# One transfer over 128 partitions in place of two over 64, for four tiles of the neighbourhood heads

## The chip, the cores and the metric

The kernel runs on one core of one Trainium2 chip. The metric is the device time of one execution in microseconds, median of several runs. The engines are TensorE (PE; its weight loads are listed as PEld), VectorE (DVE), ScalarE (ACT), GpSimd (POOL) and SyncE (SP). In this kernel SP computes nothing: its queue issues the transfers that the program asks for, one after the other, and 16 DMA engines carry them out.

## What is computed

The reference is one layer of a diffusion trunk: a SwiGLU half step, two attentions on one normalised input (neighbourhood attention and latent attention) that are merged through gates, and a second SwiGLU half step. The change touches the neighbourhood attention alone. For each of its 8 heads, each of 1024 latent queries attends in one softmax to a window of a 16 x 64 grid, with a relative bias, and to all 256 context tokens:

```python
qg, kg, vg = grid(q * d ** -0.5), grid(k), grid(v)
...
s_loc = jnp.einsum('bjqhd,bjakhd->bhjqak', q_r, k_b).astype(jnp.float32) + bias.astype(jnp.float32)
s_loc = jnp.where(valid[:, :, None, :], s_loc, neg).reshape(B, H, n_blk, NA_QCOLS, n_loc)
s_ctx = jnp.einsum('bjqhd,bkhd->bhjqk', q_r, k_ctx).astype(jnp.float32)
p = jax.nn.softmax(jnp.concatenate([s_loc, s_ctx], axis=-1), axis=-1).astype(v.dtype)
p_loc = p[..., :n_loc].reshape(B, H, n_blk, NA_QCOLS, kh, NA_KCOLS)
o = (jnp.einsum('bhjqak,bjakhd->bjqhd', p_loc, v_b)
     + jnp.einsum('bhjqk,bkhd->bjqhd', p[..., n_loc:], v_ctx))
```

A head is 64 wide (`d`). Everything is float32.

## The kernel before

To reach float32 accuracy, the kernel splits each operand into a high and a low part. A head is only 64 wide, and TensorE contracts over 128 partitions, so the two parts of a key lie one above the other: partitions 0 to 63 of the tile `k` hold the high part of the keys, 64 to 127 the low part. The tile `q` holds the high part of the queries twice, in both halves, and `ql` their low part twice. So `q` against `k` gives high times high plus high times low in one matmul. `kvc[:, 0:256]` holds the context keys, high over low like `k`.

An earlier stage computes these operands and stores them in DRAM scratch: `qas[i]`, of shape [2, 128, 1024], has the high and low queries of the two heads 2i and 2i+1, and `kas[i]`, of shape [2, 128, 1280], their keys, the last 256 columns being those of the context (L1363 and L1364). `NaHead.loads` (L1719) brings them back, head by head. It is a generator with four stages, and `na_next(h, n)` (L1885) moves it on:

- first, `q`, `ql`, the context keys and `k` (L1721 to L1730), and bias table 0;
- then bias table 1 and two blocks of values (one tile `va`);
- then bias table 2 and the context values;
- then two more blocks of values (one tile `vb`).

A head is worked off in four items (`NaItem`, L1972), one for each block of 16 grid columns. An item's `scores` (L1976) multiplies `q` and `ql` by `kvc` and by `k` into PSUM, adds the bias on VectorE and takes the maxima; its exponentials follow on ScalarE; its `values` transposes the probabilities on TensorE and multiplies them by the values.

The order is written out by hand, and each engine keeps it. Step n of the main loop (L2230) issues the three value parts of item n and between them the scores of item n + 3 (`AHEAD`). The scores of items 0 to 2 (`EARLY`) already run in the projection stage before. The first loads of head h + 1 are issued in the program at step 4h (`ahead_head`, L2190), the rest as its items 0 and 2 are created (`na_item`, L2150). Heads 0 and 1 are loaded out of the planned stage before (L1913, L1914).

Buffers limit how far the loads run ahead. The pool `w` has six tiles for `q`, `ql` and `k`: two heads. `kvc` lies in one of two `kc` tiles, or for every third head in `x`. Bias tables have three tiles (`y`), and values go round five tiles (of `l`, `p` and `z`). Every transfer is issued by SP in program order (`ld`, L122, and `put`, L131, at L132), so a load that waits for its buffer holds back all that stand behind it in SP's queue. Stores of the projection stage (`d<-t` in the views) stand in the same queue.

After the 8 neighbourhood heads the same loop works off 8 latent heads (`MlaHead`, L2060), whose loads the change doesn't touch.

## Time and profile before

| | us |
|---|---|
| median of 3 runs | 2557.08 |
| lowest and highest run | 2555.43 and 2558.92 |
| span of the profiled execution, first to last instruction | 2553.0 |

The profiled execution's own time is its span and what lies around it; the median of the runs is 4.1 us above the span. In the page, the 40 slices are of 63.8 us each. The neighbourhood heads are loaded and worked off between about 1289 and 1475 us, in slices 21 to 24. TensorE was granted its full clock throughout (0.999).

In the views, `w` stands for the tiles `q`, `ql` and `k` of a head, `kc` and `x` for its context keys, `y` for bias tables, `p`, `z` and `l` for values, `d` for DRAM scratch and `t` and `xu` for tiles of 512 and 1024 columns. KB are of 1024 bytes, MB and GB of powers of ten. All transfers are issued at line L132, the helper.

### The profile page before, as it was taken

The numbers are of one execution on the slowest core, as the hardware profiler recorded it, in microseconds if no ns is written. First come the engines' busy times: TensorE is split into PE (matmuls) and PEld (weight loads), VectorE is DVE, ScalarE is ACT, GpSimd is POOL, SyncE is SP. The second block draws the span as 40 slices with busy tenths as digits, with TensorE's granted clock in tenths as the row PEclk, the third lists the DMA queues.
The fourth block names the chain that finished last, engine by engine and source line by source line (L and its number), as shares of the span: only waits on it lengthen the run. The fifth ranks groups of instructions, "written<-read, shape, count | busy, mean of one in ns | idle before, by whom it ended". The sixth has DMA issues, their size and how long they took to land.

```text
span 2553.0 us, 38188 instructions
## 1 busy us (share of the span) xinstructions
PE 2524.7 (99%) x13007; PEld 2146.5 (84%) x13007; DVE 1904.4 (75%) x3652; ACT 1238.4 (49%) x2384; POOL 239.4 (9%) x421
## 2 busy tenths in 40 slices
PE   8999999999999999999999999999999999999998
PEld 6888888888888888889889999988888888888887
DVE  5788887898567687874568988886445888777557
ACT  6622223555346643433438888772355322233633
POOL 1000000000002200001006622220030000000000
PEclk9999999999999999999999999999999999999999
DMA  8477765779576665666899823205135667557655
GB/s 314 161 244 234 243 224 188 274 247 294 182 241 221 245 224 188 226 229 203 277 284 249 233 67 77 77 28 214 67 131 179 212 223 236 183 185 259 240 202 194
DMA packets 275477, 523.33 MB, mean 205 GB/s; under 512 B 33425, under 2 KB 84433, under 8 KB 275281
## 3 DMA queue, kind: packets, MB, share of 16 engines
q1 hardware_dynamic: 275280, 520.88, 61.3%
q8 instruction: 103, 1.69, 0.3%
q14 instruction: 94, 0.76, 0.1%
HBM read 375.47 MB, written 145.29 MB: 204 GB/s over the span
## 4 chain that ended last, share of the span: by engine, by line
PE 87%; ACT 5%; DVE 4%; issue 2%; DMA 1%; SPq 0%; POOL 0%; DVEq 0%; POOLq 0%; ACTq 0%
PE bs L161 33%; PE bm L161 30%; PE bv L161 20%; PE bm L164 2%; ACT xu L2105 2%; PE bs L164 1%; DVE xu L1966 1%; DVE t L2132 1%; ACT t L2131 1%; ACT xu L2004 1%; DVE xv L120 1%; DMA xv<-in_wada 0%; ACT t L2105 0%; ACT t L1938 0%; PE bv L164 0%
## 5 line engine op out<-in xcount | busy, mean ns | idle before, releaser
L120 ACT CAST xu<-t 128x512 fp32r<-128x512 f32 x589 | 345.6, 618 | 669.8 <-DVE t L120 556.1
L161 PE MATMUL bm<-xu,xu 128*128 128x512 f32 (+1 forms) x2442 | 596.5, 389 | 0.5 <-ACT t L120 0.4
L161 PEld LDWEIGHTS bm<-xu,xu 128*128 128x128 f32 x2442 | 450.4, 188 | 91.6 <-ACT t L120 1.7
L120 DVE TENSOR_TENSOR xu<-t,xu 128x512 fp32r<-128x512 f32 x589 | 382.8, 686 | 78.3 <-ACT xu L120 78.0
L161 PE MATMUL bs<-xu,xu 128*128 128x512 f32 (+2 forms) x1581 | 388.4, 385 | 0.0
L161 PE MATMUL bs<-xv,xu 128*128 128x512 f32 x1512 | 363.6, 390 | 0.2 <-DVE t L120 0.2
L161 PEld LDWEIGHTS bs<-xu,xu 128*128 128x128 f32 x1581 | 291.9, 188 | 57.8
L161 PE MATMUL bv<-xv,xu 128*128 128x512 f32 x1342 | 336.1, 390 | 0.0
L161 PEld LDWEIGHTS bs<-xv,xu 128*128 128x128 f32 x1512 | 283.6, 188 | 59.5 <-issue 1.0
L161 PEld LDWEIGHTS bv<-xv,xu 128*128 128x128 f32 x1342 | 251.7, 188 | 51.9
L120 DVE TENSOR_TENSOR xu<-xu,xu 128x512 fp32r<-128x512 f32 x282 | 189.5, 687 | 59.9 <-ACT xu L120 58.9
L120 DVE TENSOR_TENSOR t<-t,t 128x512 f32<-128x512 f32 (+4 forms) x350 | 221.0, 634 | 13.9 <-ACT t L120 8.7
L161 PE MATMUL bv<-xu,xu 128*128 128x512 f32 x722 | 191.5, 390 | 0.0
L120 ACT CAST xu<-xu 128x512 fp32r<-128x512 f32 x282 | 169.2, 619 | 15.2 <-DMA xu<-in_f1w 8.9
L120 POOL TENSOR_SCALAR st<-st 128x1 f32<-128x1 f32 x56 | 23.8, 425 | 1581.9 <-ACT t L120 1234.4
L161 PEld LDWEIGHTS bv<-xu,xu 128*128 128x128 f32 x722 | 135.6, 188 | 28.0
L161 PE MATMUL bm<-t,xu 128*128 128x256 f32 (+1 forms) x920 | 156.9, 333 | 0.0
L161 PEld LDWEIGHTS bm<-t,xu 128*128 128x128 f32 x920 | 137.7, 189 | 18.3
L161 PE MATMUL bs<-w,w 96*128 96x512 f32 (+1 forms) x384 | 145.0, 406 | 3.9 <-DVE st L1995 2.1
L2132 DVE TENSOR_TENSOR t<-bm,t 128x512 fp32r<-128x512 f32 x160 | 109.6, 687 | 28.5 <-ACT t L2131 28.1
L164 PE MATMUL bm<-ident,xu 128*128 128x128 f32 x826 | 126.5, 272 | 0.0
L1966 DVE TENSOR_SCALAR_CACHE_REDUCE xu<-bs 128x512 f32<-128x512 f32 (+1 forms) x186 | 110.2, 599 | 2.3 <-PE bs L161 2.1
(256 smaller groups left out, 3376.3 us busy)
## 6 DMA issues: line engine op xcount, KB each, us to landing
d<-t SPq DMA_DIRECT2D x432, 256.0 KB, 2.9
t<-d SPq DMA_DIRECT2D x348, 256.0 KB, 4.9
xu<-in_f1w SPq DMA_DIRECT2D x104, 512.0 KB, 4.4
xu<-in_f2w SPq DMA_DIRECT2D x58, 512.0 KB, 4.6
t<-in_wada SPq DMA_DIRECT2D x112, 256.0 KB, 4.9
t<-in_f1w SPq DMA_DIRECT2D x77, 256.0 KB, 4.8
t<-in_f2w SPq DMA_DIRECT2D x77, 256.0 KB, 5.2
xu<-in_winT SPq DMA_DIRECT2D x36, 512.0 KB, 5.4
```

Of the source, the lines that this page charges most:

```text
L120: return lambda *x, **y: pin(f(*x, **y))
L161: return pin(nc.tensor.matmul(o, s, m, start=start, stop=stop, skip_group_check=open_group[0]))
L164: return pin(nc.tensor.transpose(o, x, i))
L1966: nc.vector.tensor_scalar(dst, src, 1.0, FMIN, op0=ALU.mult, op1=ALU.max, accum_out=m)
L2004: soft.append(lambda s=s: nc.scalar.activation(pr[s][:, :640], pr[s][:, :640], AF.Exp, bias=n_[:, s:s + 1], accum_out=l[:, s:s + 1]))
L2105: nc.scalar.activation(x, x, AF.Exp, bias=n_[:, s:s + 1], accum_out=l[:, i:i + 1])
L2131: nc.scalar.copy(t[0], pb)
L2132: nc.vector.tensor_tensor(t[1], pb, f32(t[0]), op=ALU.subtract)
```

## The change

```diff
             self.kvc = kvc = W(key="x" if h % 3 == 2 else "kc")
-            for s in range(2):
-                o = 64 * s
-                ld(f32(q[o:o + 64, :]), qas[i][0, b:b + 64, :])
-                ld(f32(ql[o:o + 64, :]), qas[i][1, b:b + 64, :])
-                ld(f32(kvc[o:o + 64, 0:256]), kas[i][s, b:b + 64, NLAT:])
-            for s in range(2):
-                ld(f32(k[64 * s:64 * s + 64, :]), kas[i][s, b:b + 64, :NLAT])
+            for s, x in enumerate((q, ql)):
+                ld(f32(x), qas[i][s:s + 1, b:b + 64, :].to_broadcast([2, 64, NLAT]))
+            ld(f32(kvc[:, 0:256]), kas[i][:, b:b + 64, NLAT:])
+            ld(f32(k), kas[i][:, b:b + 64, :NLAT])
             self.bias = []
             self.table(0)
```

Eight transfers a head become four. The same bytes land in the same places. Each new transfer writes all 128 partitions of a tile from a source of three dimensions, two by 64 by the columns. For `q` and `ql` the outer dimension of two is a repetition: the same 64 rows are read twice. For `k` and the context keys it goes from the high part to the low part in `kas`. The order changes a little: the context keys' transfer used to be the third and the sixth, and is now the third of four, ahead of `k`.

## The prediction

> **What bounds the kernel now.** I read the page first, for the whole and for the place of the change:

> ```profile
> span 2553.0 us, 38188 instructions
> ...
> PE 2524.7 (99%) x13007; PEld 2146.5 (84%) x13007; DVE 1904.4 (75%) x3652; ACT 1238.4 (49%) x2384; POOL 239.4 (9%) x421
> ...
> DMA  8477765779576665666899823205135667557655
> GB/s 314 161 244 234 243 224 188 274 247 294 182 241 221 245 224 188 226 229 203 277 284 249 233 67 77 77 28 214 67 131 179 212 223 236 183 185 259 240 202 194
> ```

> TensorE is busy for 99% of the span: overall it sets the time. But slices 21 to 23 (1276 to 1467 us) have their DMA engines at 8 to 9 tenths, and that is where the neighbourhood heads are loaded. So the second view is that of the windows: a stretch at the start in which the DMA engines are saturated by whole tiles, and the stretch of the heads.

> ```profile
> core 0: us, PE busy (x) PEld busy (x) DVE busy (x) ACT busy (x) POOL busy (x), PEclk, DMA share, GB/s
> 3.00:43.00 40.00, 32.73 (x307) 24.00 (x308) 17.51 (x37) 20.41 (x37) 3.83 (x4) 1.00 1.03 397
> 1310.00:1450.00 140.00, 133.10 (x987) 126.91 (x986) 119.66 (x408) 112.67 (x267) 81.14 (x156) 1.00 0.92 247
> 1344.00:1445.00 101.00, 94.58 (x747) 92.32 (x746) 92.37 (x318) 90.67 (x221) 71.15 (x134) 1.00 0.98 256
> ```

> Two readings. TensorE idles for 140 - 133.1 = 6.9 us in the heads' 140 us, so nothing that only makes loads quicker can gain more than that here. And the DMA engines are as busy as can be (0.98) though they move only 256 GB/s, against 397 GB/s at the start: some transfers of this stage are slow for their size. The stage is balanced between TensorE and the DMA engines, so a change of either kind could show.

> Third, the timeline of SP's queue and of TensorE's weight loads, and the views of waits, tell how early the loads come:

> ```profile
> 1288.80 1.14 SPq L132 DMA_DIRECT2D w<-d  x2
> ...
> 1307.42 1.25 SPq L132 DMA_DIRECT2D w<-d  x2
> ...
> 1345.41 1.09 SPq L132 DMA_DIRECT2D w<-d  x2
> ...
> 1358.80 1.43 SPq L132 DMA_DIRECT2D w<-d  x2
> ```

> ```profile
> 1309.75 0.31 PEld L161 LDWEIGHTS bs<-kc,w 128*128 128x128 f32 x2
> ...
> 1355.86 0.30 PEld L161 LDWEIGHTS bs<-x,w 128*128 128x128 f32 x2
> 1358.09 0.30 PEld L161 LDWEIGHTS bs<-w,w 128*128 128x128 f32 x2 [1.92 <-DVE t L2027]
> ...
> 1373.12 0.30 PEld L161 LDWEIGHTS bs<-kc,w 128*128 128x128 f32 x2
> 1389.57 0.30 PEld L161 LDWEIGHTS bs<-kc,w 128*128 128x128 f32 x2
> ...
> 1437.18 0.30 PEld L161 LDWEIGHTS bs<-kc,w 128*128 128x128 f32 x2
> ```

> ```profile
> PE bs L161 <- DMA w<-d: 1.7, 1, 1.7
> ...
> SPq L132 <- DMA w<-d: 14.6, 21, 1.3
> ```

> Heads 0 to 3 are first loaded at 1288.80, 1307.42, 1345.41 and 1358.80 and first used at 1309.75 (head 0), 1355.86 (head 2), 1373.12 (head 3), 1389.57 (head 4) and 1437.18 (head 7). From head 3 on a head takes (1437.18 - 1373.12) / 4 = 16.0 us, and its load has 1373.12 - 1358.80 = 14.3 us to land. TensorE waited once for `w`, 1.7 us, at head 2: there is slack, but of 10 to 14 us only. SP in turn waits 21 times for landings of `w`, so its issues cannot run far ahead of slow transfers.

> **The change part by part.**

> *Issues.* Eight become four a head. SP gives about 0.6 us to each (two in 1.14 to 1.43 us), so its queue is relieved by some 2.4 us a head. SP is off the chain here. Should the three-dimensional source make an issue dearer, even twice 0.6 us leaves the sum as it was. I count nothing, either way.

> *Bytes.* They stay: 3 x 512 KB for `q`, `ql`, `k` and 128 KB of context keys, 1664 KB a head.

> *Engines.* Each new transfer has an outermost source dimension of 2 where the old ones had 64 rows. No transfer of before has one so small, so the price must be bounded. Shape does matter to speed here: the window above needs 0.98 of 16 engines for 256 GB/s. A head's other loads are 3 x 384 + 4 x 256 + 128 = 2304 KB, all over 128 partitions; at 397 GB/s they take 5.9 us of the 16.0 x 0.98 = 15.7 us that the engines are busy, which leaves 9.8 us for the 1664 KB in 64-row transfers, 174 GB/s, less than half of what whole tiles get. If a transfer is dealt to the engines by its outermost dimension, the source of 2 can be dealt to two engines and no more: one copies the upper half, the other the lower. One engine carries 397 / 16 = 24.8 GB/s. The bounds are 16 engines (1664 KB in 4.3 us, quicker than now) and 2 engines at that rate. I take two engines, since the outermost dimension is what the edit changes and the nearest rows, those of 64-row transfers, already show that fewer outer rows cost speed with all engines occupied.

> [...]

> *The sum.* On each of the two engines, a head's own load is 3 x 64 rows of 4096 bytes at 24.8 GB/s, 3 x 10.6 us, and 64 rows of 1024 bytes, 2.6 us: 34.3 us. All four transfers use the same two engines and follow each other. Those two also carry their sixteenth of everything else:

> ```profile
> q1 hardware_dynamic: 16417, 35.75, 92.4%
> ...
> w<-d SPq DMA_DIRECT2D x48, 256.0 KB, 7.3
> y<-in_bias SPq DMA_DIRECT2D x21, 384.0 KB, 5.5
> d<-t SPq DMA_DIRECT2D x24, 256.0 KB, 4.3
> ```

> ```profile
> t<-d SPq DMA_DIRECT2D x10, 128.0 KB, 2.2
> ```

> The first fence is the view of transfers in the window from head 0's first load to head 7's last, 1288.7 to 1428.6 (packets, MB and the engines' share; then count, KB each and us to landing). The second, of the whole span, is the quickest landing among its transfers of 128 KB or more, 2.2 us, which I take for the time between issue and landing that isn't copying. In that window 35.75 MB move, of which 8 x 1.704 MB are the edited loads; a sixteenth of the other 22.1 MB is 1.38 MB, 55.7 us of one engine. A steady head adds 2304 KB / 16 at 24.8 GB/s, 5.9 us.

> Head by head: head 0 issued at 1288.8 has landed at 1288.8 + 2.2 + 34.3 = 1325. The stores and loads between it and head 1 (12 stores of 256 KB and 1792 KB of tables and values) add 12.5 us, head 1 its 34.3: 1372. Between head 1 and 2 stand 12 more stores and 2816 KB: 15.2 + 34.3, so 1421. Then each head takes 34.3 + 5.9 = 40.2 us, and head 7 has landed at 1421 + 5 x 40.2 = 1622. The check by totals: 1288.8 + 2.2 + 8 x 34.3 + 55.7 = 1621. Its bias table 0 comes behind on the same engines, 1 us. Head 7 was first used at 1437.18, so TensorE, in written order, gets there 1623 - 1437 = 186 us later. No slack is left to subtract: while it waits it has nothing else. A head's work (16 us) fits into the next one's load (40 us), so only loads add up. Two heads of `w` are enough: head h + 1's tiles are free once head h - 1's scores are done, long before head h has landed.

> Behind head 7 the latent heads' loads find their buffers free and 16 engines, so nothing is added there: 2553.0 + 186 = 2739 for the span of the profiled execution, and with the 4.1 us by which the median lies above it, 2743.

> **The rivals.**

> *Sixteen engines* (not slower): the outer 2 is merged or split on the way to the engines, and 1664 KB land at 397 GB/s, in 4.3 us in place of 9.8. For it: the bytes written are the same whole tiles that reach 397 GB/s at the start. Against: the source is not one even run of rows. What it gains is head 2's wait,

> ```profile
> 1349.74 8.24 DMA w<-d
> ```

> a piece of the chain that ended last: `k` of head 2 lands at 1357.98. It would come some 5 us sooner, but the tiles' first users wait no more than 1.9 us there, and the heads after it are not waiting for loads. 2557 - 2 = 2555; all 6.9 us idle would be 2550. It decides if a transfer spreads by its 128 rows written.

> *Two engines, but other ones for each transfer:* the four run beside each other in 10.6 + 2.2 us. Head 2's `k` issued near 1347 would land at 1360 for 1358, the later heads keep within 14.3 us: 2559. The rows don't say how engines are chosen.

> *Two engines at the slow rate:* if what slows 64-row transfers (174 / 16 = 10.9 GB/s an engine) holds for these too, a head's own load is 78 us, and 8 x 78 + 56 us end at 1971: 2557 + 534 = 3091. Against it: that rate was seen with sixteen engines at once on 64 partitions; two are unlikely to stand in each other's way.

> **How the numbers follow.** Two engines, the same for all: 0.83. Sixteen: 0.11. Different pairs: 0.03. The slow rate: 0.03. The predicted time is the first's, 2743. Its own low end has all other traffic beside the loads: 8 x 34.3 + 2.2 from 1288.8 is 1565, +128 us, 2685. Its high end has the other traffic at this stage's 256 GB/s (22.1 MB in 86 us, 30 us more) and an unhidden issue-to-landing time of `w` (7.3 us) for each of seven heads, 51 us: 2743 + 81 = 2824. I widen to 2680 and 2840 for stalls that the stores cause in the projection stage. A measurement here can tell about 0.2%, 5 us, from no change. Slower: 0.83 and 0.03, 0.86. Within: different pairs and most of sixteen engines, 0.03 + 0.08 = 0.11. Faster: 0.03, sixteen engines with nearly all the idle time regained.

> **What would show it.** The DMA line of the page falls to about two or three tenths of busy share in the heads' stretch, at some 100 GB/s (4.07 MB in 40 us). `w<-d` of 512 KB lands 10 us and more after its issue, later ones of a head over 30. First uses of successive heads lie 40 us apart, and TensorE's largest waits are for `w<-d`, about 24 us each. SP's loads of head h + 1 stand behind landings of head h. The median sits near 2743 with no loss elsewhere. I am wrong if `w<-d` lands in under 7 us (sixteen engines), if the four loads of a head land together (different pairs), or if a head takes near 80 us.

## The result, and the profile after

The changed kernel takes 2752.29 us in the median (2751.14 to 2754.93) against 2556.63 us before in the same runs: 195.7 us more, a ratio of 1.077 with a 95% interval of 1.0756 to 1.0783. The forecast was 2743. The span of its profiled execution is 2751.3 us.

The page of the changed kernel, in the lines shown of before:

```profile
span 2751.3 us, 38156 instructions
...
PE 2547.8 (93%) x13007; PEld 2165.0 (79%) x13007; DVE 1904.7 (69%) x3652; ACT 1240.5 (45%) x2384; POOL 239.5 (9%) x421
...
DMA  8567766787656656677433243220524466655855
GB/s 303 188 218 249 235 214 217 274 274 230 219 214 240 217 199 220 220 203 274 153 118 107 91 121 96 73 72 26 207 84 165 168 218 230 206 176 202 317 177 191
```

A slice is now 68.8 us. Where slices 21 to 23 of before had DMA shares of 8 to 9 tenths, slices 20 to 24 now have 2 to 4, at 91 to 153 GB/s: less is moved at a time and the stretch is longer. Outside it, the line is as before.

The windows of the heads' stretch, then of one head from the issue of its `q` to that of the next (1464.9 to 1508), cut by what the DMA engines do:

```profile
core 0: us, PE busy (x) PEld busy (x) DVE busy (x) ACT busy (x) POOL busy (x), PEclk, DMA share, GB/s
1440.00:1600.00 160.00, 63.88 (x421) 61.83 (x422) 50.90 (x175) 51.02 (x120) 39.29 (x75) 0.68 0.32 99
...
1467.50:1488.00 20.50, 14.43 (x109) 14.19 (x108) 14.33 (x50) 14.51 (x35) 11.67 (x22) 0.92 0.13 51
1488.00:1493.60 5.60, 0.00 (x0) 0.00 (x0) 0.00 (x0) 0.00 (x0) 0.00 (x0) 0.50 0.37 118
1493.60:1506.50 12.90, 0.77 (x2) 0.50 (x2) 0.00 (x0) 0.00 (x0) 0.00 (x0) 0.50 0.57 154
```

The second row is the plainest reading of the case. While `q` and `ql` move, the DMA share is 0.13: two engines of sixteen are 0.125. They carry 51 GB/s, 25.5 each. Next to nothing else moves, though the other fourteen are free. TensorE does the work of the head before in these 20 us and then all but stands still for the next 18.5, at a granted clock of 0.50.

The timeline of TensorE's weight loads, with the first use of `k` by heads 0, 1, 2 and 3, of the context keys by head 7 and of `k` by head 7 (in brackets how long the engine sat idle before it); then TensorE's waits in the stretch (us in total, times, longest):

```profile
1324.96 0.50 PEld L161 LDWEIGHTS bs<-w,w 128*128 128x128 f32 x2 [10.60 <-issue]
...
1371.17 0.50 PEld L161 LDWEIGHTS bs<-w,w 128*128 128x128 f32 x2 [9.51 <-issue]
...
1421.72 0.50 PEld L161 LDWEIGHTS bs<-w,w 128*128 128x128 f32 x2 [11.47 <-issue]
...
1463.96 0.50 PEld L161 LDWEIGHTS bs<-w,w 128*128 128x128 f32 x2 [11.68 <-issue]
...
1622.47 0.50 PEld L161 LDWEIGHTS bs<-kc,w 128*128 128x128 f32 x2 [12.88 <-issue]
1634.60 0.50 PEld L161 LDWEIGHTS bs<-w,w 128*128 128x128 f32 x2 [11.62 <-issue]
```

```profile
PE bs L161 <- DMA w<-d: 87.6, 8, 11.5
PE bs L161 <- DMA kc<-d: 32.6, 3, 12.7
PE bs L161 <- issue: 30.0, 3, 13.1
PE bs L161 <- DMA x<-d: 29.7, 2, 17.0
```

TensorE waits twice a head: for the context keys, the third load, and again for `k`, the fourth: 12.9 and 11.6 us at head 7. The four rows of waits make 180 us. From head 2 on, heads follow each other every (1634.60 - 1421.72) / 5 = 42.6 us, where they took 16.0. Head 7's scores start 1622.47 - 1437.18 = 185 us later than before, and its `k` comes 12 us after that: there is the whole loss.

SP's queue shows something that was not foreseen. In the timeline of its issues (start, time that the issue took):

```profile
1422.68 1.49 SPq L132 DMA_DIRECT2D w<-d  x2
1424.29 3.86 SPq L132 DMA_DIRECT2D kc<-d  x1
1428.20 17.03 SPq L132 DMA_DIRECT2D w<-d  x1
```

`q` and `ql` are issued in 1.49 us together, but the two loads behind them take 3.86 and 17.03 us to issue. So there was a second way to read the result: that SP, not the DMA engines, is slow with such transfers. The experiments begin there.

### The profile page after: what moved, and what is told of

The parts are those of the page before. It is cut to its first block, busy times and chain, and to the rows that moved or that the text cites. A ratio compares the mean times of both kernels' runs of the same rounds, so it can differ in the third digit from the quotient of the medians.

```text
span 2751.3 us, 38156 instructions
## 1 busy us (share of the span) xinstructions
PE 2547.8 (93%) x13007; PEld 2165.0 (79%) x13007; DVE 1904.7 (69%) x3652; ACT 1240.5 (45%) x2384; POOL 239.5 (9%) x421
## 4 chain that ended last, share of the span: by engine, by line
PE 77%; DMA 8%; SPq 5%; ACT 4%; DVE 3%; issue 2%; POOL 0%; DVEq 0%; POOLq 0%; ACTq 0%
PE bs L161 30%; PE bm L161 26%; PE bv L161 18%; SPq L132 5%; DMA w<-d 2%; ACT xu L2102 2%; DMA p<-d 1%; DMA z<-d 1%; PE bm L164 1%; PE bs L164 1%; DVE xu L1963 1%; ACT t L2128 1%; DVE t L2129 1%; DVE xv L120 1%; DMA l<-d 1%
## 5 line engine op out<-in xcount | busy, mean ns | idle before, releaser
L161 PE MATMUL bm<-xu,xu 128*128 128x512 f32 (+1 forms) x2442 | 596.3, 388 | 0.4 <-ACT t L120 0.2
L161 PEld LDWEIGHTS bm<-xu,xu 128*128 128x128 f32 x2442 | 450.0, 188 | 91.7 <-ACT t L120 1.6
L161 PE MATMUL bs<-xu,xu 128*128 128x512 f32 (+2 forms) x1581 | 388.3, 384 | 0.0
L161 PE MATMUL bs<-xv,xu 128*128 128x512 f32 x1512 | 363.5, 389 | 0.2 <-DVE t L120 0.2
L161 PEld LDWEIGHTS bs<-xu,xu 128*128 128x128 f32 x1581 | 291.7, 188 | 58.0
L161 PE MATMUL bv<-xv,xu 128*128 128x512 f32 x1342 | 336.0, 389 | 0.0
L161 PEld LDWEIGHTS bs<-xv,xu 128*128 128x128 f32 x1512 | 283.5, 188 | 59.7 <-issue 1.0
L161 PEld LDWEIGHTS bv<-xv,xu 128*128 128x128 f32 x1342 | 251.6, 188 | 52.1
L161 PE MATMUL bs<-w,w 96*128 96x512 f32 (+1 forms) x384 | 150.4, 422 | 87.8 <-DMA w<-d 87.6
L161 PE MATMUL bv<-xu,xu 128*128 128x512 f32 x722 | 191.4, 389 | 0.0
L161 PEld LDWEIGHTS bv<-xu,xu 128*128 128x128 f32 x722 | 135.5, 188 | 28.1
L161 PE MATMUL bm<-t,xu 128*128 128x256 f32 (+1 forms) x920 | 156.9, 332 | 0.0
L1992 DVE CUSTOM_DVE_ANT_0 xu<-bs,y 128x384 f32<-128x384 f32 x58 | 31.3, 550 | 178.9 <-PE bs L161 175.2
L161 PEld LDWEIGHTS bm<-t,xu 128*128 128x128 f32 x920 | 137.5, 189 | 18.5
L161 PEld LDWEIGHTS bs<-w,w 96*128 96x128 f32 (+1 forms) x384 | 71.3, 199 | 97.1 <-issue 89.7
## 6 DMA issues: line engine op xcount, KB each, us to landing
d<-t SPq DMA_DIRECT2D x432, 256.0 KB
t<-d SPq DMA_DIRECT2D x348, 256.0 KB
t<-in_wada SPq DMA_DIRECT2D x112, 256.0 KB
t<-in_f1w SPq DMA_DIRECT2D x77, 256.0 KB
t<-in_f2w SPq DMA_DIRECT2D x77, 256.0 KB
```

The source lines that it names most:

```text
L161: return pin(nc.tensor.matmul(o, s, m, start=start, stop=stop, skip_group_check=open_group[0]))
L1992: nc.vector.tensor_tensor_reduce(out=pr[s][:, :384], in0=loc[:, :384], in1=hd.bias[BVAR[j]][:, s * 384:(s + 1) * 384], scale=1.0, scalar=FMIN,
```

## The experiments

**The outer dimension alone.** `rows_outer` keeps the four transfers, their three-dimensional sources, the repetition and the bytes, and turns the two outer dimensions round, so that the two copies of a row, or the high and low part of a key row, lie side by side (partitions 2r and 2r + 1):

```diff
-                ld(f32(x), qas[i][s:s + 1, b:b + 64, :].to_broadcast([2, 64, NLAT]))
-            ld(f32(kvc[:, 0:256]), kas[i][:, b:b + 64, NLAT:])
-            ld(f32(k), kas[i][:, b:b + 64, :NLAT])
+                ld(f32(x), qas[i][s, b:b + 64, :].rearrange("r (o c) -> r o c", o=1).to_broadcast([64, 2, NLAT]))
+            ld(f32(kvc[:, 0:256]), kas[i][:, b:b + 64, NLAT:].rearrange("s r c -> r s c"))
+            ld(f32(k), kas[i][:, b:b + 64, :NLAT].rearrange("s r c -> r s c"))
```

A score is a sum over the 128 partitions of a query and a key, so their order is free as long as queries and keys have the same.

> The same four transfers over 128 partitions, with the 64 rows as the outer dimension of the source and the 2 inside (partition 2r + s in place of 64s + r, for queries and keys alike). Theory 'outer dimension': a transfer is dealt to the DMA engines by its outermost source dimension, so 64 gives all sixteen; a head's 1664 KB land at up to 397 GB/s, the loss of 196 us is gone, and with head 2's wait of 1.7 us gone too 2550 to 2557 us. Rival 'issue': a three-dimensional source is slow to issue (SP took 7 to 17 us over single loads after the change), whatever its order: some 2750 us again. Rival 'repetition': reading the same rows twice (outer stride 0) is what is slow: queries still slow, above 2650 us.

Measured: 2551.2 us against 2555.85, ratio 0.9983 (0.9974 to 0.9992). The loss is gone whole, with the same number of issues and sources that still have three dimensions; SP issues head 2's `q` and `ql` in 1.17 us together and `k` in 0.60. So neither the three dimensions nor the repetition made the changed kernel slow; its outer dimension of 2 did. The result is even a little faster than the kernel before. Its window of the stretch that the prediction showed of before, and TensorE's waits there:

```profile
1310.00:1450.00 140.00, 136.94 (x1013) 130.42 (x1013) 121.48 (x419) 114.74 (x272) 82.78 (x159) 1.00 0.71 241
```

```profile
PE bs L161 <- DMA w<-d: 1.7, 1, 1.7
PE bs L161 <- DVE st L1992: 1.0, 4, 0.5
```

and of before, the wait for the same VectorE instruction (L1995 there):

```profile
PE bs L161 <- DVE st L1995: 5.1, 5, 2.6
```

The DMA share falls from 0.92 to 0.71 while the rate is about the same (241 and 247 GB/s): in this stage whole tiles cost the engines less than halves. The trace also records every packet with its start, duration and bytes; a row of 4096 bytes, as only `q`, `ql` and `k` have between 1310 and 1440 us, takes 0.18 us on average there in place of 0.30. TensorE idles for 140 - 136.94 = 3.1 us in place of 6.9. The wait for `w` at head 2 is the same 1.7 us, only 2 us earlier; what shrinks is the wait for VectorE's reductions, from 5.1 to 1.0 us. The longest of these, 2.6 us, ends at 1348 us, ahead of head 2. There VectorE has its instructions in another order, first before, then in `rows_outer`:

```profile
1343.37 0.69 DVE L2027 TENSOR_TENSOR t<-bm,t 128x512 fp32r<-128x512 f32 x1
...
1347.36 0.55 DVE L1995 CUSTOM_DVE_ANT_0 xu<-bs,y 128x384 f32<-128x384 f32 x1
```

```profile
1344.52 0.69 DVE L2024 TENSOR_TENSOR t<-bm,t 128x512 fp32r<-128x512 f32 x1
1345.12 0.55 DVE L1992 CUSTOM_DVE_ANT_0 xu<-bs,y 128x384 f32<-128x384 f32 x1
```

In `rows_outer` the reduction follows at once; before, five other operations stood between. The edit names no VectorE instruction, and that each engine keeps the written order holds for TensorE alone: its 13007 matmuls stand in the same order in the traces of before and of the changed kernel, while 149 of VectorE's 3652 instructions and 101 of ScalarE's 2384 do not. So the gain is real (3.8 us of idle time, 4.6 us in the medians), but whether it comes from the quicker transfers or from this order stays open. The changed kernel has the order of `rows_outer`, so the loss between these two owes nothing to it.

**Queries alone, keys alone.** If the two engines are the bound, the loss must go with the bytes that are sent through them.

```diff
 queries_only: q and ql by the two new loads; kvc and k as before:
+            for s in range(2):
+                ld(f32(kvc[64 * s:64 * s + 64, 0:256]), kas[i][s, b:b + 64, NLAT:])
+            for s in range(2):
+                ld(f32(k[64 * s:64 * s + 64, :]), kas[i][s, b:b + 64, :NLAT])
 keys_only: kvc and k by the two new loads; q and ql as before:
+                ld(f32(q[o:o + 64, :]), qas[i][0, b:b + 64, :])
+                ld(f32(ql[o:o + 64, :]), qas[i][1, b:b + 64, :])
```

> Only q and ql are loaded the new way (outer 2), context keys and k as before in two halves. Theory 'outer dimension': a head's load on the two engines falls from 34.3 to 2 x 10.6 = 21.2 us, 640 KB in halves take 3.8 us (174 GB/s), the rest 8.3 us (42.6 us between heads after the change, less 34.3): 33.3 us a head, 9.3 less in each of 8 heads than after the change, 2752 - 74 = 2678 us. Rival 'repetition': the whole loss stays, some 2750 us. If keys alone were slow: 2557 us.

> Only context keys and k are loaded the new way, q and ql as before in two halves. Theory 'outer dimension': 10.6 + 2.6 = 13.2 us on the two engines, 1024 KB in halves 6.0 us (174 GB/s), the rest 8.3: 27.5 us a head, 15.1 less in each of 8 heads than after the change, 2752 - 121 = 2631 us. Rival 'repetition' (these sources repeat nothing): 2557 us.

Measured: queries alone 2670.69 us (ratio 1.0444, 1.043 to 1.0458), keys alone 2630.62 us (1.0292, 1.0276 to 1.0308), for 2678 and 2631 worked out. Keys, which repeat nothing, have their share of the loss. The two losses, 114.8 and 74.8 us, add up to 189.6, near the 195.7 of the whole.

**How many engines.** Is the outer dimension an upper limit on the engines, or must their number divide it? Three kernels take `rows_outer` and cut each transfer into one of 62 and one of 2 rows, of 61 and 3, of 60 and 4:

```diff
+            for x, y in ((0, 62), (62, 64)):
+                for s, z in enumerate((q, ql)):
+                    ld(f32(z[2 * x:2 * y, :]),
+                       qas[i][s, b + x:b + y, :].rearrange("r (o c) -> r o c", o=1).to_broadcast([y - x, 2, NLAT]))
+                ld(f32(kvc[2 * x:2 * y, 0:256]), kas[i][:, b + x:b + y, NLAT:].rearrange("s r c -> r s c"))
+                ld(f32(k[2 * x:2 * y, :]), kas[i][:, b + x:b + y, :NLAT].rearrange("s r c -> r s c"))
```

> As rows_outer, but each transfer is cut into one of 62 rows (124 partitions) and one of 2 rows (4 partitions). If the outer dimension caps the engines by its size, 62 is enough for sixteen: about 2557 us. If the engines' count has to divide it (62 = 2 x 31), only two engines serve both pieces, with the same rows each as after the change: some 2750 us. [...]

> As rows_62_2, cut into 61 and 3 rows. 61 is a prime: if the count of engines must divide the outer dimension, one engine carries 122 partitions of each tile: 3 x 122 x 0.165 + 122 x 0.041 = 65.4 us, with the three rows (two partitions on each of three engines) 66.5 us a head. 1288.8 + 2.2 + 8 x 66.5 + 55.7 = 1879 for head 7's load, and some 19 us as after the change (8 x 2.4): 1898, 461 us later than 1437: about 3015 us. If the size of the dimension capped the engines: 2557 us.

> As rows_62_2, cut into 60 and 4 rows, the same number of transfers as there. 60 = 15 x 4: by the divisor fifteen engines, and four for the short piece: near rows_outer, 2550 to 2557 us. If cutting the tiles, or the short piece, is what made rows_62_2 slow: 2700 us and more.

Measured: 2746.77 us for 62 (1.0746, 1.0726 to 1.0765), 2993.7 us for 61 (one run), 2556.78 us for 60 (1.0006, 0.9995 to 1.0016). A row or two decide between no loss, 191 us and 438 us (459 were worked out for 61). An outer dimension of 62 is as slow as one of 2 (2746.77 and 2752.29 us), 61 is slower than both (2993.7), as it must be if the number of engines divides the outer dimension: two for 62 and one for the prime 61; for 60 it can be fifteen. The traces agree. First the window of `rows_62_2` and, for comparison, of the changed kernel, then the DMA line of `rows_61_3` between 1500 and 1700 us:

```profile
1350.00:1600.00 250.00, 105.18 (x735) 102.79 (x734) 91.90 (x311) 88.28 (x211) 65.74 (x127) 0.71 0.33 112
```

```profile
1350.00:1600.00 250.00, 105.65 (x696) 100.92 (x695) 85.88 (x295) 84.90 (x200) 62.18 (x120) 0.70 0.34 111
```

```profile
DMA  4207000000000015053000000000060260000000
GB/s 164 88 26 270 26 30 26 25 26 25 26 25 23 26 44 209 26 185 112 29 29 26 25 26 25 26 23 24 31 219 30 75 221 25 31 25 26 25 26 25
```

62 rows move as 2 do (0.33 and 0.34 of the engines, 112 and 111 GB/s). With 61 rows most slices are at 25 to 26 GB/s, one engine's rate, a share of 0.06 that the line rounds to 0. The control with 60 and 4 rows has as many transfers as the other two and loses nothing, so neither the cut nor the short pieces are to blame. The packets show the number of engines as well: where rows of 4096 bytes are in progress at all, it is most often 1 of them at a time with 61 rows (1500 to 1700 us), 2 with 62 and in the changed kernel (both 1350 to 1600 us), 15 with 60 and 16 in `rows_outer` (both 1350 to 1430 us).

The three kernels have VectorE's instructions in the order of before. With 60 rows the DMA share between 1310 and 1450 us is still 0.90, so this run has neither of the two things that may have made `rows_outer` faster, and cannot tell them apart.

**The 2.4 us a head that the sum lacked.** The sum had 40.2 us a head, the trace 42.6. Two causes were open: an idle piece of the two engines between `k` of one head and `q` of the next, which SP issues late, or a loss among the other loads. `next_first` changes the order of issue on the changed kernel:

```diff
-            na_next(h, 1 if j else 2)
+            na_next(h, 0 if j else 2)
...
             heads["mla", h - NH] = MlaHead(h - NH)
+        if 1 < h <= NH:
+            na_next(h - 1)
```

> The changed kernel with one more edit: a head's last two value loads (tile vb) are issued behind the first loads of the next head in place of ahead of them. After the change heads follow each other every 42.6 us where 34.3 + 5.9 = 40.2 were worked out. Theory 'handover': the 2.4 us are an idle piece of the two engines, because SP gives out the next head's q only once k of the head before has landed (it waits for that landing at the value loads). With q ahead of that wait it is in the queue early: 40 us between heads, 5 to 7 times 2.4 us less, 2735 to 2740 us. Rival 'mixed traffic': the two engines lose the 2.4 us among the other loads that they carry in between; then the order does nothing, 2752 us.

Measured: 2750.24 us (1.0762, 1.0748 to 1.0777), 2 us below the changed kernel, with intervals that overlap. That looks like the second cause, but the trace shows that the edit did not do what it was made for. The first use of `k` by a head and the issue of the next head's `q`:

```profile
1461.82 0.50 PEld L161 LDWEIGHTS bs<-w,w 128*128 128x128 f32 x2 [11.55 <-issue]
```

```profile
1462.75 1.63 SPq L132 DMA_DIRECT2D w<-d  x2
```

The next head's `q` is still issued after `k` has landed and is in use. `values_merged` does away with that: with two value loads in place of four, two loads fewer stand between.

```diff
-    vws = [DR([NH, P, 512]) for _ in range(4)]
+    vws = [DR([NH, P, 1024]) for _ in range(2)]
...
-            for j in range(2):
-                self.values(va, j)
+            self.values(va, 0)
...
-            o = (j % 2) * 512
-            ld(f32(v[:, o:o + 512]), vws[j][self.h])
+            ld(f32(v), vws[j][self.h])
```

> The changed kernel with the four value loads of a head (128 x 512 each) as two of 128 x 1024, from a scratch laid out so. In next_first q of the next head was still issued behind the landing of k (1462.75 after 1461.82), since eight other loads stand between them, so it did not put the question. With six between them q can be issued before k has landed. Theory 'handover' (the 2.4 us a head over the 40.2 worked out are an idle piece of the two engines between k and the next q): 40 us between heads, 2735 to 2740 us. Rival 'mixed traffic' (the two engines are never idle and lose time among the other loads): 42 us between heads, 2748 to 2752 us, though q is issued early.

Measured: 2754.0 us (1.0779, 1.0764 to 1.0794). In its timelines, the issue of `q` and `ql`, and the first use of `k` by heads 2, 3 and 7:

```profile
1457.15 9.21 SPq L132 DMA_DIRECT2D w<-d  x2
```

```profile
1421.58 0.50 PEld L161 LDWEIGHTS bs<-w,w 128*128 128x128 f32 x2 [11.99 <-issue]
...
1464.16 0.50 PEld L161 LDWEIGHTS bs<-w,w 128*128 128x128 f32 x2 [12.09 <-issue]
...
1636.44 0.50 PEld L161 LDWEIGHTS bs<-w,w 128*128 128x128 f32 x2 [12.87 <-issue]
```

`q` is now issued 7 us before `k` of the head before is used (1457.15 and 1464.16), and heads follow each other every (1636.44 - 1421.58) / 5 = 43.0 us, no sooner. Early issue buys nothing: the handover is not the cause (the merge also changes the rows of the value loads, so this run is not the early issue alone). The changed kernel's DMA line over one head (1464.9 to 1508) fits that:

```profile
DMA  8111111111111111111111111799746783821112
GB/s 249 52 50 42 42 53 49 61 49 53 53 49 57 53 49 53 49 53 49 53 49 52 48 46 48 205 340 290 162 106 220 166 253 112 211 89 52 52 48 61
```

There is no slice below 42 GB/s, about the rate of two engines. What remains is that the two engines take longer than 5.9 us over their sixteenth of the other loads, or over their own rows beside them. The packets of the changed kernel decide for the second. While `q` and `ql` move alone, a row takes 0.162 us (median, 1470 to 1487 us). When the other engines move tables and values (1493.5 to 1503 us), the rows of `k` take 0.21 us on average, and 0.16 again when that is over. Over heads 3 to 7 the rows of `k` average 0.200 us. Each of the two engines copies 64 of them, so a head loses 64 x (0.200 - 0.162) = 2.4 us: the time that the sum lacked. Why a row takes longer beside other traffic is not shown.

**The better version with fewer loads.** The same merge on `rows_outer`:

> rows_outer with the same merge of the value loads. TensorE waits for no load of a head in rows_outer, so two issues fewer a head are worth nothing: as rows_outer, 2549 to 2554 us. If SP's queue were what holds the heads at 16 us each, some 8 x 1 us less: 2543 us.

Measured: 2551.05 us (0.9985, 0.9976 to 0.9994), the same as `rows_outer`. SP's queue was not what spaces the heads there. Of these two, `rows_outer` is the simpler.

## Why the prediction was right

*What bounds the stretch.* Right: the slack of 10 to 14 us was used up and the DMA engines became the bound of the stretch.

*Issues.* Counted at nothing. SP's issues became far longer, 17.03 us for one, and still cost nothing of their own: the three-dimensional sources of `rows_outer` bring back the old time, and an earlier issue in `values_merged` gains none. Why they are long is not shown.

*Engines.* Right, and the step that carries everything: two engines, the same two for all loads. The share of 0.13 and 51 GB/s show two, and that a head's loads follow each other shows that they are the same two. The rate taken was 24.8 GB/s an engine, from the first 40 us of the trace of before; the trace after gives 25.5. But the reason given for choosing two engines over sixteen was only half right. That the edit changes the outermost dimension was the point. That the 64-row transfers of before "already show that fewer outer rows cost speed" does not hold: `rows_outer` has 64 outer rows too and is quick (0.18 us a row of 4096 bytes, the halves 0.30). What slows the halves is something else about them, and no run isolates it. That this reason, too, pointed at two engines was luck.

*The sum.* Heads 0, 1 and 2 were to have landed at 1325, 1372 and 1421; their `k` is used at 1325.0, 1371.2 and 1421.7. Then each head takes 42.6 us where 40.2 were worked out. The mis-sized term is the copying of the three tiles, 3 x 10.6 = 31.8 us: over heads 3 to 7 each engine's 192 rows take 34.0 us, since those of `k` are slower beside the other loads (0.200 us a row, where 24.8 GB/s give 0.165). Over five heads the 2.4 us are 12, and `k` of head 7 is used at 1634.6 for 1622. The span misses by as much, 2751.3 for 2739. The median misses by 9 only, 2752 for 2743, because the 4.1 us by which it was to lie above the span came to 1.0; those 3 us are luck.

*The range.* The measured time lies well inside. The high end allowed 30 us for slower other traffic; what became slower was the tiles' own copying, by less.

*Rivals.* "Sixteen engines" did not happen here but could be built: `rows_outer` is that case. Its price was 2555, and it came to 2551: the gain was sought in head 2's wait for its load, which stayed at 1.7 us, and was found in shorter waits for VectorE, whose cause is open. "Other engines for each transfer" falls with the two waits a head, which show the loads landing one after the other. "The slow rate" (10.9 GB/s an engine) falls with 25.5 GB/s.

*What would show it.* The DMA share of two to three tenths at some 100 GB/s was 0.32 at 99. TensorE's wait of about 24 us a head is there, but in two parts, 12.9 us for the context keys and 11.6 us for `k` at head 7.

## What to carry to other kernels

Before merging transfers, look at the outer dimension of the merged source: here two halves stacked as an outer 2 (repeated or not) were moved by two engines of sixteen, as were 62 rows, while 61 rows were moved by one, 60 by fifteen and 64 by sixteen. If the order of the rows is free, put the long dimension outside; here that took away a loss of 7.7%. (The 0.2% by which the result beats the kernel before may not come from the transfers at all: the order of VectorE's instructions changed as well.) And a load that lands in time with 10 us of slack can still become the bound of its whole stage when it is moved at an eighth of the width (a DMA share of 0.13 here).

## What was not expected of the hardware

An issue was not always short: SP spent up to 17.03 us on one instruction that issues a load to the two busy engines (from 1428.20 us), where two issues of loads of `w` took 1.14 us before, and the next issue in its queue started at 1445.33, right behind it.

A row of the same size took an engine longer while the others were at work: 0.162 us (median) for 4096 bytes when the two engines move alone, 0.21 us on average when the others move tables and values beside them. So in this stage the two engines lost more to the other traffic than its bytes: 2.4 us a head.

TensorE's granted clock was lower where it waited: 0.50 in the windows where it stands still, 0.68 over 160 us of the stretch, against 1.00 before. The weight loads right after a wait came in pairs of 0.50 us in place of 0.30. As long as a longer wait for a load follows (11.6 us at head 7), this adds nothing; what it costs behind the last head's wait was not measured.
